# Two indexer units advanced together behind 13 products of ones, reversed queries for a small bias table, and h fetched four chunks ahead

## The chip, the core and the metric

The kernel runs on one core of a Trainium2 chip. A core has five engines that run their own instruction streams and meet at semaphores: TensorE (PE, matrix products; its weight loads are listed apart as PEld), VectorE (DVE), ScalarE (ACT), GpSimd (POOL) and SyncE (SP, which here only issues transfers). Products read SBUF and write PSUM, which has eight banks of 128 x 512 fp32. The metric is the device time of one execution in microseconds (us).

## The reference, cut to what matters

Two layers act on x (256 tokens, width 2048). Layer 0 multiplies the normalised x by one wide weight matrix whose columns feed an RG-LRU recurrence and a sparse attention; layer 1 is a gated MLP. After each layer a gated per-layer embedding is added to the residual h.

```python
# layer 0, attention: an indexer scores every key for every query, 64 keys are kept
s_h = relu(einsum('bqhd,bsd->bqhs', iqb, ik))              # 16 indexer heads of 64
score = einsum('bqhs,bqh->bqs', s_h, iwb) * idx_scale      # iw: a weight per query and head
score = where(key_pos < (q_pos // 64 + 1) * 64, score, -inf)
_, sel = top_k(score, 64)
logits = einsum('bqgrd,bqkgd->bqgrk', qg, kg) * att_scale  # 16 heads of 128, 4 kv heads
bias = rel_table[t5_bucket(sel - q_pos)]                   # depends on key - query and head alone
probs = softmax(logits + bias)
o = einsum('bqgrk,bqkgd->bqgrd', probs, vg)
# each layer
h = h + mix
h = h + sigmoid(rms_norm(h) @ w_gate) * (p_i @ w_pe)
```

## The kernel before

Weights come from HBM in chunks of 128 rows by two k tiles by 512 columns (368 for the indexer). For each chunk SP issues a load (L147), ACT rounds the weights to `hi` (L155), DVE computes the rest `lo = raw - hi` (L156), and PE multiplies: the activations are split the same way, and each k tile and half of the tokens takes three products in fp32r, hi by xh, lo by xh and hi by xl (L189 to L191), so 12 products to a chunk. `unit` makes the chunks of one 512-column block; `spair` and `half_pair` make blocks with seven instead of eight multiplications (tiles U, V, W, Z), whose chunks are half as long.

`program` appends all chunks to one list and walks it. At chunk j it issues loads (at most 13 raw buffers) and splits up to three chunks ahead (`feed`), then chunk j's products, and then `advance` lets every background task go one step, up to its next `yield`. A task does what lies around the products: it takes finished PSUM tiles, transposes, scores, scans. A scheduler then sets each engine's final order from what tasks and chunks issue; each engine executes its own in order. `spawn(task, n)` delays a task by n steps.

Names that the change and the prediction touch:

- `fm` (L437): four 128 x 128 transpositions on PE, `nc.tensor.transpose` with an identity; used with tiles iqt (indexer queries), qt (queries), kt, ht, ybt and more. In `head_pair` three more a head transpose the softmax numerators (tile pt, L735).
- `idx_task`, `iq_task`: take the indexer's three 368-column units (key `ik`, weight `iw`, 16 query heads `iq`), then per step two products pairs `sc` (L589), relu on ACT and weighted sums on DVE; `topk` makes the mask.
- `bias_table`: a product makes a 16 x 384 table of head by (key - query); ACT writes it 128 times, each row shifted by one, to an HBM scratch of 3 MB (L493). `head_pair` reads a 128 x 2 x 256 tile of it (L695).
- `fetch` and `add_h_task`: h lies in HBM between the gate of layer 0 and layer 1; when a block of layer 1's output projection ("y") is complete, `add_h_task` issues the fetch (L917), and adds a step later (L926), and `to_acts` transposes the sum (ht) a step after that.
- the lead of `program`: loads and splits of the first three chunks and of all eight x tiles before the walk.

The lines most spoken of:

```python
437  def fm(self, a0, a1, name="fm"):
443      self.nc.tensor.transpose(pt[...], x[:, k * 128:(k + 1) * 128], self.ident)
571  nc.scalar.activation(iq, pt, AF.Copy)             # iqT
735  nc.tensor.transpose(pt[:, o:o + 128], L[h][:, c:c + 128], self.ident)
744  nc.tensor.matmul(po[:, o0:o0 + 128], PT[h][:, 0:128], self.v[0][:, kv], start=True, stop=True)
917  self.nc.sync.dma_start(h, self.hd[c, t])
926  self.nc.vector.tensor_tensor(hs[t], ps[t], hs[t], op=OP.add)
1057 nc.tensor.matmul(pm[:, s], self.ws[c][:, i], self.ov[c, t][:, s], start=True, stop=True)
```

Of the kernel before, what the change touches and what calls it, by code (L numbers as in the profile page):

```python
# [27 lines left out]
T = 256  # L28
# [3 lines left out]
H = 16  # L32
# [37 lines left out]
class Chunk:  # L70
    def __init__(self, ap, cols, mm, half=False):
        self.ap, self.cols, self.mm, self.half = ap, cols, mm, half
        self.prev = self.next = self.raw = self.hl = None
        self.spawn = []
# [7 lines left out]
class Trunk:  # L82
# [259 lines left out]
    def half_stage(self, key, prev, acts, task, *args, before=None, lead=4, tail=3):  # L342
# [4 lines left out]
        def rest(i):  # L347
            def f(ps):
                st["h%d" % i] = []
                for t in range(2):  # L350
# [10 lines left out]
                            [self.post(task, c, *args) for c in (0, 1)], first)  # L361
        ss = ss[:10] + pre(1) + [None, None] + ss[10:12] + pre(0) + [None, None] + ss[12:]
# [14 lines left out]
        self.chunks += cs  # L377

# [58 lines left out]
    def fm(self, a0, a1, name="fm"):  # L437

        pt = self.pa(name)
        with self.tc.issue_after(self.last_mm.ins):  # L440
            for k in range(2):
                for t, x in ((0, a0), (1, a1)):
                    self.nc.tensor.transpose(pt[:, k * T + t * 128:k * T + (t + 1) * 128],  # L443
                                             x[:, k * 128:(k + 1) * 128], self.ident)
# [21 lines left out]
    def consts(self):  # L466
# [3 lines left out]
        self.ident = self.kept([128, 128], "ident")  # L470
        nc.gpsimd.dma_start(self.ident, a["ident"])
# [3 lines left out]
        nc.scalar.activation(warm, self.mhalf, AF.Tanh)  # L475
        self.r = {}

    def bias_table(self):
# [7 lines left out]
        with self.tc.issue_after(self.last_mm.ins):  # L486
            nc.tensor.matmul(ps[:H, :N_BUCKET_COLS], rel, oh, start=True, stop=True)
        sb = self.kept([H, N_BUCKET_COLS], "bt")
        nc.scalar.activation(sb, ps[:H, :N_BUCKET_COLS], AF.Copy)

        bd = self.bias_d = self.dram.tile([H, 128, 512], F32, name="bias_d")
        yield
        nc.scalar.dma_start(bass.AP(tensor=bd.tensor, offset=bd.offset, ap=[[128 * 512, H], [513, 128], [1, 383]]),  # L493
                            sb[:, None, :383].to_broadcast([H, 128, 383]))
# [31 lines left out]
    def idx_task(self, i, ps):  # L526
# [3 lines left out]
        if i == 0:  # L530
# [16 lines left out]
            with self.tc.issue_after(self.last_mm.ins):  # L547
                for t in range(2):
                    nc.tensor.transpose(pt[:, t * 128:(t + 1) * 128], ikd[t], self.ident)
            self.ik = self.t([128, T], name="ik")  # L550
# [13 lines left out]
    def iq_task(self, j):  # L564
# [4 lines left out]
        pt = self.fm(self.iq[j // 2][0][:, o:o + T], self.iq[j // 2][1][:, o:o + T], "iqt")  # L569
# [31 lines left out]
    def topk(self):  # L601
        nc = self.nc
        sc = self.score
        nc.vector.memset(sc[0:64, 192:256], OUT_OF_RANGE)
        nc.vector.memset(sc[0:64, 320:384], OUT_OF_RANGE)
# [62 lines left out]
    def q_task(self, g, ps):  # L668
# [5 lines left out]
        rq = self.kept([128, 2, 4], "rq")  # L674
        nc.vector.tensor_scalar(rq, ss, 128 * EPS, None, op0=OP.add)
        nc.gpsimd.tensor_tensor(self.flat(rq), self.flat(rq), self.mhalf, op=OP.pow)
        self.rq[g] = rq
        qT = []
        for p in range(2):
            pt = self.fm(qs[0][:, p * T:(p + 1) * T], qs[1][:, p * T:(p + 1) * T], "qt")  # L680
# [3 lines left out]
        yield  # L684
        yield from self.until("mask", "k", "v", "bias")
# [4 lines left out]
    def head_pair(self, g, p, qT):  # L690
# [4 lines left out]
        nc.gpsimd.dma_start(bt, bass.AP(tensor=bd.tensor, offset=bd.offset + h0 * 128 * 512 + 127,  # L695
                                        ap=[[512, 128], [128 * 512, 2], [1, T]]))
# [31 lines left out]
        rc = self.sm([128, 4])  # L728
        nc.vector.reciprocal(rc, sm)
        for i, t in ((0, 1), (1, 0)):  # L730
            nc.vector.tensor_scalar(rc[:, 2 * i:2 * i + 2], rc[:, 2 * i:2 * i + 2], self.rth("x", t), None, op0=OP.mult)
        for h in range(2):
            pt = self.pa("pt")
            for o, c in ((0, 256), (128, 0), (256, 128)):
                nc.tensor.transpose(pt[:, o:o + 128], L[h][:, c:c + 128], self.ident)  # L735
            x = self.t([128, 384], name="PT")
            nc.scalar.activation(x, pt[:, :384], AF.Copy)
            PT.append(x)
        yield
# [172 lines left out]

    def fetch(self, c):
# [6 lines left out]
    def add_h_task(self, c, layer, ps):  # L920
        if layer == 1:
            self.fetch(c)
            yield
# [189 lines left out]
    def program(self):  # L1113
# [9 lines left out]
        for i in range(3):  # L1123
            self.put(self.unit([a["idx_w"][i, :, o * 736:(o + 1) * 736] for o in range(8)], xs,
                               self.post(self.idx_task, i), n=368))
# [43 lines left out]

# [155 lines left out]
```

## Time and profile before

| | us |
|---|---|
| median of 3 timed runs | 1246.75 (1245.07 to 1247.82) |
| the profiled execution | 1248.01 |
| its span (first to last instruction) | 1246.2 |
| PE busy | 1227.4 (98%) |
| DVE busy | 944.3 (76%) |
| ACT busy | 785.0 (63%) |

The profile comes from one execution. Busy time of PE counts a product until its result is out, so products overlap in it; how fast PE goes is read from start to start. The rest of the profiled execution, 1.8 us, lies around the span. All numbers of the rows below are from this execution.

### The profile page before, as it was taken

To read this page: it belongs to the slowest core of one execution; us is meant where nothing else is said; L and a number is where in the kernel's file an instruction comes from. 1 tells how busy PE (TensorE), PEld (TensorE's weight loads), DVE (VectorE), ACT (ScalarE), POOL (GpSimd) and SP (SyncE) were. 2 spreads that over 40 slices of the span, in tenths; PEclk is the share of its full clock that TensorE was granted. 3 is DMA by queue.
4 is the path that set the end of the run, shared out by engine and by line. 5 is a ranking of instruction groups with operands and counts; after the bars stand their busy time and mean duration, and the time that the engine had idled before them with its cause. 6 is when DMAs were issued, how large, how long until landed. Compare 5 with 4: busy or idle time off the path is not lost.

```text
span 1246.2 us, 16543 instructions
## 1 busy us (share of the span) xinstructions
PE 1227.4 (98%) x5780; PEld 1023.8 (82%) x5780; DVE 944.3 (76%) x1487; ACT 785.0 (63%) x1099; POOL 147.4 (12%) x178
## 2 busy tenths in 40 slices
PE   7999999999999999999999999999999999999998
PEld 7978887888888888888888888788888888887886
DVE  6779658786677778775568877887899778677865
ACT  6755546664477878863466776676765656565753
POOL 0001131412000001000110110032112000100100
PEclk9999999999999999999999999999999999999999
DMA  9997997636546555576787798889999965986961
GB/s 345 253 249 231 299 219 240 227 128 199 183 157 201 172 186 177 178 239 216 188 246 250 187 291 281 225 241 271 274 274 277 279 222 156 244 267 203 261 186 43
DMA packets 82868, 279.31 MB, mean 224 GB/s; under 512 B 9264, under 2 KB 11968, under 8 KB 82784
## 3 DMA queue, kind: packets, MB, share of 16 engines
q1 hardware_dynamic: 66672, 225.18, 52.0%
q0 software_dynamic: 14048, 49.94, 21.2%
q10 hardware_dynamic: 2064, 3.14, 1.9%
q8 instruction: 45, 0.74, 0.2%
q14 instruction: 39, 0.32, 0.1%
HBM read 270.89 MB, written 7.33 MB: 223 GB/s over the span
## 4 chain that ended last, share of the span: by engine, by line
PE 89%; DMA 5%; DVE 3%; issue 2%; ACT 1%; SPq 0%; POOL 0%; DVEq 0%; ACTq 0%
PE pg L191 22%; PE pg L189 22%; PE pg L190 22%; DMA bias_d<-bt 3%; PE U L229 1%; PE U L231 1%; PE U L230 1%; DVE lo L156 1%; ACT hi L155 1%; PE ht L443 1%; PE Z L230 1%; PE Z L229 1%; PE Z L231 1%; PE V L230 1%; PE U L290 1%
## 5 line engine op out<-in xcount | busy, mean ns | idle before, releaser
L156 DVE TENSOR_TENSOR lo<-raw,hi 128x1024 fp32r<-128x1024 f32 (+1 forms) x492 | 587.6, 1212 | 201.5 <-ACT hi L155 197.2
L155 ACT ACTIVATE hi<-raw 128x1024 fp32r<-128x1024 f32 (+1 forms) x492 | 511.5, 1048 | 350.2 <-PE pg L191 256.0
L189 PE MATMUL pg<-hi,xh 128*128 128x512 f32 (+1 forms) x1376 | 536.9, 390 | 6.8 <-ACT xh L426 6.3
L190 PE MATMUL pg<-lo,xh 128*128 128x512 f32 (+1 forms) x1376 | 532.0, 387 | 0.5 <-DVE lo L156 0.5
L191 PE MATMUL pg<-hi,xl 128*128 128x512 f32 (+1 forms) x1376 | 531.9, 387 | 0.5 <-DVE xl L427 0.4
L189 PEld LDWEIGHTS pg<-hi,xh 128*128 128x128 f32 x1376 | 259.5, 189 | 57.6 <-ACT xh L426 6.9
L191 PEld LDWEIGHTS pg<-hi,xl 128*128 128x128 f32 x1376 | 259.0, 188 | 51.7 <-DVE xl L427 1.6
L190 PEld LDWEIGHTS pg<-lo,xh 128*128 128x128 f32 x1376 | 259.5, 189 | 49.1 <-DVE lo L156 1.0
L160 POOL DMA_DIRECT2D raw<-in_w7h x32 | 27.7, 866 | 357.3 <-DMA raw<-in_w 197.5
L160 POOL DMA_DIRECT2D raw<-in_w x48 | 41.8, 892 | 203.7 <-DVE lo L156 110.6
L426 ACT ACTIVATE xh<-ht,cols 128x256 fp32r<-128x256 f32 x48 | 22.0, 469 | 19.1 <-DVE xl L427 11.9
L803 POOL TENSOR_TENSOR tt<-tt,tg 128x512 f32<-128x512 f32 x8 | 10.3, 1294 | 183.1 <-ACT tt L801 164.3
L229 PE MATMUL U<-hi,xh 128*128 128x512 f32 x72 | 29.0, 403 | 0.0
L231 PE MATMUL U<-lo,xh 128*128 128x512 f32 x72 | 28.1, 390 | 0.0
L230 PE MATMUL U<-hi,xl 128*128 128x512 f32 x72 | 28.1, 390 | 0.0
L427 DVE SCALAR_TENSOR_TENSOR xl<-ht,cols,xh 128x256 fp32r<-128x256 f32 x48 | 22.6, 481 | 5.7 <-ACT xh L426 5.6
L725 ACT ACTIVATE L<-L,s 128x256 f32<-128x256 f32 (+1 forms) x32 | 14.3, 448 | 15.5 <-DVE s L719 14.8
L434 DVE TENSOR_TENSOR xl<-s,xh 128x512 fp32r<-128x512 f32 x32 | 22.0, 687 | 1.9 <-ACT xh L433 1.9
L433 ACT ACTIVATE xh<-s 128x512 fp32r<-128x512 f32 x32 | 19.9, 622 | 4.8 <-DVE s L414 4.7
L717 DVE SCALAR_TENSOR_TENSOR L<-lg,rq,bm 128x256 f32<-128x256 f32 (+1 forms) x32 | 12.0, 410 | 14.4 <-POOL bm L702 12.4
L829 DVE SCALAR_TENSOR_TENSOR xc<-xat,cols,xc 128x255 f32<-128x255 f32 (+2 forms) x48 | 22.2, 477 | 0.5
L231 PE MATMUL V<-lo,xh 128*128 128x512 f32 x48 | 18.8, 391 | 0.5 <-DVE lo L156 0.5
(310 smaller groups left out, 1346.9 us busy)
## 6 DMA issues: line engine op xcount, KB each, us to landing
raw<-in_w SPq DMA_DIRECT2D x356, 512.0 KB, 5.0
raw<-in_w POOLq DMA_DIRECT2D x48, 512.0 KB, 8.7
raw<-in_w7h POOLq DMA_DIRECT2D x32, 512.0 KB, 7.1
raw<-in_w7h SPq DMA_DIRECT2D x24, 512.0 KB, 4.4
raw<-in_idx_w SPq DMA_DIRECT2D x24, 368.0 KB, 7.4
raw<-in_pe_w SPq DMA_DIRECT2D x8, 512.0 KB, 6.0
bias_d<-bt ACTq DMA_DIRECT2D x1, 3064.0 KB, 35.9
x<-in_xT SPq DMA_DIRECT2D x8, 256.0 KB, 7.3
```

Source lines behind the costliest of these rows:

```text
L155: nc.scalar.activation(hi[:, :c.cols], raw, AF.Copy)
L156: self.last_lo = nc.vector.tensor_tensor(lo[:, :c.cols], raw, hi[:, :c.cols].bitcast(F32), op=OP.subtract)
L160: nc.gpsimd.dma_start(c.raw, c.next.ap, accum_op=OP.add)
L189: self.nc.tensor.matmul(ps, xh, wh, start=(c == order[0] and k == 0), stop=False)
L190: self.nc.tensor.matmul(ps, xh, wl, start=False, stop=False)
L191: self.last_mm = self.nc.tensor.matmul(ps, xl, wh, start=False, stop=(c == order[-1] and k == 1))
L229: nc.tensor.matmul(st[b], ah, wh, start=new and k == 0, stop=False, skip_group_check=True)
L230: nc.tensor.matmul(st[b], al, wh, start=False, stop=False, skip_group_check=True)
L231: self.last_mm = nc.tensor.matmul(st[b], ah, wl, start=False, stop=(c == order[3] and k == 1), skip_group_check=True)
L426: nc.scalar.activation(hi[:, s], src[:, s], AF.Copy, scale=g)
L427: nc.vector.scalar_tensor_tensor(lo[:, s], src[:, s], g, hi[:, s].bitcast(F32), op0=OP.mult, op1=OP.subtract)
L829: nc.vector.scalar_tensor_tensor(xc[:, s, k:], xa[:, s, :T - k], col(C_CW + (3 - k) * 16 + f), xc[:, s, k:], op0=OP.mult, op1=OP.add)
```

## The change

- Lead: a tile of ones is set on DVE, and 13 products of it (128 x 512, fp32r) stand at the head of PE's order. Loads are queued x tile by x tile with two weight chunks each; ten are issued ahead; x tiles are split as the walk comes to them.
- Indexer: the chunks of its first two units alternate, so that both use the same x tile one after the other; the third unit follows. x norm and x sums start later (13 and 19 steps).
- Queries in reverse: indexer queries, queries and softmax numerators go through a plain product with a reversed identity instead of a transposition. The weights `iw` and the sums of squares `ss` and of the softmax `sm` go through small products with it, so that they come in the same order. The table is then written once (24 KB), and read with a step of one element from partition to partition.
- Fetch of h: for "y", the loads are a task of their own, started four chunks before the block's last chunk; `add_h_task` adds at once.

```diff
@@ -361,2 +361,4 @@
                             [self.post(task, c, *args) for c in (0, 1)], first)
+        cs[7].ends, ss[11].ends, ss[13].ends, cs[-1].ends = 2, 1, 0, 3
+        mark = len(self.chunks)
         ss = ss[:10] + pre(1) + [None, None] + ss[10:12] + pre(0) + [None, None] + ss[12:]
@@ -377,2 +379,6 @@
         self.chunks += cs
+        if key == "y":
+            for i in range(mark, len(self.chunks)):
+                if self.chunks[i].ends is not None:
+                    self.chunks[i - 4].spawn.append(lambda c=self.chunks[i].ends: self.fetch_task(c))
 
@@ -436,3 +442,4 @@
 
-    def fm(self, a0, a1, name="fm"):
+    def fm(self, a0, a1, name="fm", flip=False):
+
 
@@ -442,4 +449,8 @@
                 for t, x in ((0, a0), (1, a1)):
-                    self.nc.tensor.transpose(pt[:, k * T + t * 128:k * T + (t + 1) * 128],
-                                             x[:, k * 128:(k + 1) * 128], self.ident)
+                    o = pt[:, k * T + t * 128:k * T + (t + 1) * 128]
+                    x = x[:, k * 128:(k + 1) * 128]
+                    if flip:
+                        self.nc.tensor.matmul(o, x, self.flip, start=True, stop=True)
+                    else:
+                        self.nc.tensor.transpose(o, x, self.ident)
         return pt.rearrange("p (a b) -> p a b", a=2)
@@ -469,4 +480,5 @@
         nc.sync.dma_start(self.cols, a["cols"])
-        self.ident = self.kept([128, 128], "ident")
-        nc.gpsimd.dma_start(self.ident, a["ident"])
+        both = self.kept([128, 256], "ident")
+        nc.gpsimd.dma_start(both, a["ident"])
+        self.ident, self.flip = both[:, 0:128], both[:, 128:256]
         self.mhalf = self.kept([128, 8], "mhalf")
@@ -475,2 +487,7 @@
         nc.scalar.activation(warm, self.mhalf, AF.Tanh)
+        ones = self.t(name="ones")
+        nc.vector.memset(ones, 1.0)
+        ps = self.pa("warm")
+        for i in range(13):
+            nc.tensor.matmul(ps, ones[:, 0:128].bitcast(F32R), ones.bitcast(F32R), start=True, stop=True)
         self.r = {}
@@ -487,9 +504,8 @@
             nc.tensor.matmul(ps[:H, :N_BUCKET_COLS], rel, oh, start=True, stop=True)
-        sb = self.kept([H, N_BUCKET_COLS], "bt")
+        sb = self.t([H, N_BUCKET_COLS], name="bt")
         nc.scalar.activation(sb, ps[:H, :N_BUCKET_COLS], AF.Copy)
 
-        bd = self.bias_d = self.dram.tile([H, 128, 512], F32, name="bias_d")
+        self.bias_d = self.dram.tile([H, N_BUCKET_COLS], F32, name="bias_d")
         yield
-        nc.scalar.dma_start(bass.AP(tensor=bd.tensor, offset=bd.offset, ap=[[128 * 512, H], [513, 128], [1, 383]]),
-                            sb[:, None, :383].to_broadcast([H, 128, 383]))
+        nc.scalar.dma_start(self.bias_d, sb)
         self.done.add("bias")
@@ -549,2 +565,5 @@
                     nc.tensor.transpose(pt[:, t * 128:(t + 1) * 128], ikd[t], self.ident)
+                nc.tensor.matmul(pt[:, T:T + 2 * IH], self.flip, self.flat(self.iw), start=True, stop=True)
+            self.iw = self.kept([128, 2, IH], "iwf")
+            nc.scalar.activation(self.flat(self.iw), pt[:, T:T + 2 * IH], AF.Copy)
             self.ik = self.t([128, T], name="ik")
@@ -568,3 +587,3 @@
         o = (j % 2) * T
-        pt = self.fm(self.iq[j // 2][0][:, o:o + T], self.iq[j // 2][1][:, o:o + T], "iqt")
+        pt = self.fm(self.iq[j // 2][0][:, o:o + T], self.iq[j // 2][1][:, o:o + T], "iqt", True)
         iq = self.t([128, 2, T], name="iqT")
@@ -603,4 +622,4 @@
         sc = self.score
-        nc.vector.memset(sc[0:64, 192:256], OUT_OF_RANGE)
-        nc.vector.memset(sc[0:64, 320:384], OUT_OF_RANGE)
+        nc.vector.memset(sc[64:128, 192:256], OUT_OF_RANGE)
+        nc.vector.memset(sc[64:128, 320:384], OUT_OF_RANGE)
         for rnd in range(8):
@@ -673,9 +692,5 @@
         self.head_sums(qs, ss)
-        rq = self.kept([128, 2, 4], "rq")
-        nc.vector.tensor_scalar(rq, ss, 128 * EPS, None, op0=OP.add)
-        nc.gpsimd.tensor_tensor(self.flat(rq), self.flat(rq), self.mhalf, op=OP.pow)
-        self.rq[g] = rq
         qT = []
         for p in range(2):
-            pt = self.fm(qs[0][:, p * T:(p + 1) * T], qs[1][:, p * T:(p + 1) * T], "qt")
+            pt = self.fm(qs[0][:, p * T:(p + 1) * T], qs[1][:, p * T:(p + 1) * T], "qt", True)
             x = self.t([128, 2, T], name="qT")
@@ -684,2 +699,9 @@
         yield
+        ps = self.pa("rq")
+        with self.tc.issue_after(self.last_mm.ins):
+            nc.tensor.matmul(ps[:, 0:8], self.flip, self.flat(ss), start=True, stop=True)
+        rq = self.kept([128, 2, 4], "rq")
+        nc.vector.tensor_scalar(self.flat(rq), ps[:, 0:8], 128 * EPS, None, op0=OP.add)
+        nc.gpsimd.tensor_tensor(self.flat(rq), self.flat(rq), self.mhalf, op=OP.pow)
+        self.rq[g] = rq
         yield from self.until("mask", "k", "v", "bias")
@@ -694,4 +716,4 @@
         bd = self.bias_d
-        nc.gpsimd.dma_start(bt, bass.AP(tensor=bd.tensor, offset=bd.offset + h0 * 128 * 512 + 127,
-                                        ap=[[512, 128], [128 * 512, 2], [1, T]]))
+        nc.gpsimd.dma_start(bt, bass.AP(tensor=bd.tensor, offset=bd.offset + h0 * N_BUCKET_COLS,
+                                        ap=[[1, 128], [N_BUCKET_COLS, 2], [1, T]]))
         lg, bm, L, PT = [], [], [], []
@@ -727,6 +749,2 @@
         yield
-        rc = self.sm([128, 4])
-        nc.vector.reciprocal(rc, sm)
-        for i, t in ((0, 1), (1, 0)):
-            nc.vector.tensor_scalar(rc[:, 2 * i:2 * i + 2], rc[:, 2 * i:2 * i + 2], self.rth("x", t), None, op0=OP.mult)
         for h in range(2):
@@ -734,3 +752,5 @@
             for o, c in ((0, 256), (128, 0), (256, 128)):
-                nc.tensor.transpose(pt[:, o:o + 128], L[h][:, c:c + 128], self.ident)
+                nc.tensor.matmul(pt[:, o:o + 128], L[h][:, c:c + 128], self.flip, start=True, stop=True)
+            if h == 1:
+                nc.tensor.matmul(pt[:, 384:388], self.flip, sm, start=True, stop=True)
             x = self.t([128, 384], name="PT")
@@ -738,2 +758,6 @@
             PT.append(x)
+        rc = self.sm([128, 4])
+        nc.vector.reciprocal(rc, pt[:, 384:388])
+        for i, t in ((0, 1), (1, 0)):
+            nc.vector.tensor_scalar(rc[:, 2 * i:2 * i + 2], rc[:, 2 * i:2 * i + 2], self.rth("x", t), None, op0=OP.mult)
         yield
@@ -912,2 +936,6 @@
 
+    def fetch_task(self, c):
+        self.fetch(c)
+        yield
+
     def fetch(self, c):
@@ -920,5 +948,2 @@
     def add_h_task(self, c, layer, ps):
-        if layer == 1:
-            self.fetch(c)
-            yield
         hs = self.h[c]
@@ -1122,5 +1147,5 @@
         xs = lambda: self.xs
-        for i in range(3):
-            self.put(self.unit([a["idx_w"][i, :, o * 736:(o + 1) * 736] for o in range(8)], xs,
-                               self.post(self.idx_task, i), n=368))
+        idx = [self.unit([a["idx_w"][i, :, o * 736:(o + 1) * 736] for o in range(8)], xs,
+                         self.post(self.idx_task, i), n=368) for i in range(3)]
+        self.put(sum(map(list, zip(idx[0], idx[1])), []), idx[2])
         wu = lambda acts, task, *args, **kw: self.put(self.wunit(acts, self.post(task, *args), **kw))
@@ -1169,17 +1194,17 @@
 
+        def split_x(j):
+            if j < PAIRS and j not in self.xs:
+                self.xs[j] = self.split(x[j], self.cols[:, C_NG + 2 * j:C_NG + 2 * j + 2])
+
         with self.tc.manual_schedule():
             self.consts()
-            self.issue_load(0)
-            load_xt(0)
-            self.issue_load(1)
-            load_xt(1)
-            self.issue_load(2)
-            for j in range(2, PAIRS):
-                load_xt(j)
-            self.next_load = 3
             for j in range(PAIRS):
-                g = self.cols[:, C_NG + 2 * j:C_NG + 2 * j + 2]
-                if j in (0, 1, 3):
-                    self.feed(-1, {0: 1, 1: 2, 3: 3}[j])
-                self.xs[j] = self.split(x[j], g)
+                load_xt(j)
+                if j < 5:
+                    self.issue_load(2 * j)
+                    self.issue_load(2 * j + 1)
+            self.next_load = 10
+            for j in range(3):
+                split_x(j)
+                self.feed(-1, min(2 * j + 2, 5))
 
@@ -1204,4 +1229,4 @@
 
-        self.spawn(x_norm(), 8)
-        self.spawn(x_sums(), 16)
+        self.spawn(x_norm(), 13)
+        self.spawn(x_sums(), 19)
         self.spawn(self.bias_table(), 8)
@@ -1215,2 +1240,3 @@
                 self.spawn(mk())
+            split_x((j + AHEAD + 1) // 2)
             self.feed(j)
...
```

In the order that each engine executes, the change shows at three places. At the head of PE's order (pg are the units' PSUM tiles, hi and lo a chunk's weights, xh and xl an x tile), before:

```order
L189 MATMUL pg_184<-hi_113,xh_117 128x368
L190 MATMUL pg_184<-lo_114,xh_117 128x368
L191 MATMUL pg_184<-hi_113,xl_118 128x368
L189 MATMUL pg_184<-hi_113,xh_117 128x368
L190 MATMUL pg_184<-lo_114,xh_117 128x368
L191 MATMUL pg_184<-hi_113,xl_118 128x368
```

and now:

```order
L492 MATMUL warm_87<-ones_85 128x512 x13
L189 MATMUL pg_176<-hi_143,xh_137 128x368
L189 MATMUL pg_177<-hi_143,xh_137 128x368
L189 MATMUL pg_190<-hi_147,xh_137 128x368
L190 MATMUL pg_176<-lo_144,xh_137 128x368
L191 MATMUL pg_176<-hi_143,xl_138 128x368
L189 MATMUL pg_176<-hi_143,xh_137 128x368
L190 MATMUL pg_176<-lo_144,xh_137 128x368
```

A product of the second unit's chunk (hi_147) now stands third, ahead of the first that reads lo. 

ACT's order where the indexer's tiles are taken (ik and iqT feed the first sc products, pg_344 and pg_345 hold the second unit, pg_542 and pg_543 the third), before:

```order
L551 ACTIVATE ik_520<-ikt_517 128x256
L529 ACTIVATE iq_326<-pg_344 128x144
L529 ACTIVATE iq_327<-pg_345 128x144
L406 ACTIVATE xe_564<-x_87,cols_77 128x256
L155 ACTIVATE hi_613<-raw_480 128x736
L571 ACTIVATE iqT_577<-iqt_572 128x512
```

and now:

```order
L568 ACTIVATE iwf_641<-ikt_637 128x32
L570 ACTIVATE ik_643<-ikt_637 128x256
L439 ACTIVATE xh_663<-s_631 128x512
L545 ACTIVATE iq_495<-pg_542 128x368
L545 ACTIVATE iq_496<-pg_543 128x368
L590 ACTIVATE iqT_672<-iqt_667 128x512
```

The copy of iqT now stands behind two copies that read the third unit's finished tiles.

SP's order at the last two blocks of "y" (hr are the fetched tiles of h, raw the weights), before:

```order
L147 DMA raw_10640<-in_w 128x1024
L917 DMA hr_10340<-hd_7283 128x512
L917 DMA hr_10342<-hd_7285 128x512
L147 DMA raw_10659<-in_w7h 128x1024
L147 DMA raw_10673<-in_w 128x1024
L147 DMA raw_10703<-in_w 128x1024
L917 DMA hr_10468<-hd_7417 128x512
L917 DMA hr_10470<-hd_7419 128x512
```

and now:

```order
L147 DMA raw_10643<-in_w 128x1024
L945 DMA hr_10311<-hd_7318 128x512
L945 DMA hr_10313<-hd_7320 128x512
L147 DMA raw_10662<-in_w7h 128x1024
L945 DMA hr_10379<-hd_7452 128x512
L945 DMA hr_10381<-hd_7454 128x512
L147 DMA raw_10675<-in_w 128x1024
```

The last block's two loads moved past two weight loads, to directly behind the first load after the other block's.

## Rows read from the trace of the kernel before

**Rows 1.** The page: the span, and busy time of each engine with its instructions.
```profile
span 1246.2 us, 16543 instructions
...
PE 1227.4 (98%) x5780; PEld 1023.8 (82%) x5780; DVE 944.3 (76%) x1487; ACT 785.0 (63%) x1099; POOL 147.4 (12%) x178
```
**Rows 2.** Waits of PE: waiter <- awaited: us in total, times, longest.
```profile
PE pg L189 <- ACT xh L426: 6.3, 2, 6.1
PE sc L589 <- ACT iqT L571: 2.4, 1, 2.4
PE ht L443 <- DVE hr L926: 1.9, 3, 1.5
...
```
**Rows 3.** Groups of PE: line, out<-in, shape, xcount | busy us, mean ns | idle before.
```profile
L735 PE MATMUL pt<-ident,L 128*128 128x128 f32 x48 | 6.5, 272 | 0.0
L744 PE MATMUL o<-v,PT 128*128 128x128 f32 x32 | 6.3, 277 | 0.4 <-ACT PT L737 0.4
...
L443 PE MATMUL qt<-ident,q 128*128 128x128 f32 x24 | 3.1, 272 | 0.0
L443 PE MATMUL iqt<-ident,iq 128*128 128x128 f32 x16 | 2.4, 272 | 0.0
```
**Rows 4.** Timeline of PE around one head pair's transpositions: start us, us, what.
```profile
175.94 0.82 PE L735 MATMUL pt<-ident,L 128*128 128x128 f32 x6
...
176.83 0.40 PE L230 MATMUL U<-hi,xl 128*128 128x512 f32 x1
177.06 0.40 PE L231 MATMUL U<-lo,xh 128*128 128x512 f32 x1
```
**Rows 5.** Timeline of PE around four plain fp32 products of layer 1.
```profile
948.25 1.05 PE L1057 MATMUL mix<-v,ws 128*128 128x128 f32 x8
...
949.37 0.40 PE L230 MATMUL U<-hi,xl 128*128 128x512 f32 x1
```
**Rows 6.** Line 735: weight loads, ns min/median/max, first and last start.
```profile
L735 PEld LDWEIGHTS pt<-ident,L x48: 138/140/144, 175.7 to 335.0; 128*128 128x128 f32 x48
```
**Rows 7.** Timeline of PE at the start.
```profile
6.07 0.68 PE L189 MATMUL pg<-hi,xh 128*128 128x368 f32 x1 [6.07 <-ACT xh L426]
...
11.30 0.51 PE L190 MATMUL pg<-lo,xh 128*128 128x368 f32 x1
11.60 0.51 PE L191 MATMUL pg<-hi,xl 128*128 128x368 f32 x1
...
17.09 0.33 PE L191 MATMUL pg<-hi,xl 128*128 128x368 f32 x1
17.26 0.33 PE L189 MATMUL pg<-hi,xh 128*128 128x368 f32 x1
```
**Rows 8.** Timeline of ACT at the start.
```profile
5.50 0.91 ACT L426 ACTIVATE xh<-x,cols 128x256 fp32r<-128x256 f32 x2
6.55 0.82 ACT L155 ACTIVATE hi<-raw 128x736 fp32r<-128x736 f32 x1
...
8.95 0.91 ACT L426 ACTIVATE xh<-x,cols 128x256 fp32r<-128x256 f32 x2 [1.57 <-DMA x<-in_xT]
```
**Rows 9.** The chain that ended last, 38 to 80 and 1136 us: start us, us, what.
```profile
38.97 35.94 DMA bias_d<-bt
74.98 3.58 DMA raw<-in_w
...
1136.43 5.93 DMA hr<-hd
```
**Rows 10.** Timeline of ACT, 62 to 66 us: the third unit's copies.
```profile
64.28 0.96 ACT L529 ACTIVATE iq<-pg 128x368 f32<-128x368 f32 x2
```
**Rows 11.** Timeline of PE, 192 to 194 us.
```profile
192.88 0.40 PE L230 MATMUL V<-hi,xl 128*128 128x512 f32 x1
193.81 0.50 PE L231 MATMUL V<-lo,xh 128*128 128x512 f32 x1 [0.53 <-DVE lo L156]
```
**Rows 12.** Groups of DVE at line 926.
```profile
L926 DVE TENSOR_TENSOR hr<-h,hr 128x512 f32<-128x512 f32 x4 | 2.8, 693 | 1.6 <-DMA hr<-hd 1.5
```

More of the change, by code (lines that the diff above doesn't have):

```diff
@@ L72, in __init__ @@
         self.ap, self.cols, self.mm, self.half = ap, cols, mm, half
-        self.prev = self.next = self.raw = self.hl = None
+        self.prev = self.next = self.raw = self.hl = self.ends = None
         self.spawn = []
@@ L1168, in load_xt @@
             x.append(t)
+        def split_x(j):
+            if j < PAIRS and j not in self.xs:
+                self.xs[j] = self.split(x[j], self.cols[:, C_NG + 2 * j:C_NG + 2 * j + 2])
         with self.tc.manual_schedule():
             self.consts()
-            self.issue_load(0)
-            load_xt(0)
-            self.issue_load(1)
-            load_xt(1)
-            self.issue_load(2)
-            for j in range(2, PAIRS):
-                load_xt(j)
-            self.next_load = 3
-            for j in range(PAIRS):
-                g = self.cols[:, C_NG + 2 * j:C_NG + 2 * j + 2]
-                if j in (0, 1, 3):
-                    self.feed(-1, {0: 1, 1: 2, 3: 3}[j])
-                self.xs[j] = self.split(x[j], g)
+            for j in range(PAIRS):
+                load_xt(j)
+                if j < 5:
[5 more added lines that the diff above has]
+                self.feed(-1, min(2 * j + 2, 5))
         def x_norm():
@@ L1306, in _layout @@
         "pT": c(np.asarray(i["p"])[:, 0].reshape(2, T, 2, 128).transpose(0, 3, 2, 1)),
-        "ident": np.eye(128, dtype=np.float32),
+        "ident": np.concatenate([np.eye(128, dtype=np.float32), np.eye(128, dtype=np.float32)[::-1]], axis=1),
         "onehot": _buckets(),
```

## The prediction

> **What bounds the kernel now.** I read four views. The page's first part comes first: PE is busy for 1227.4 of a span of 1246.2 us, and the next engine, DVE, for 944.3 [rows 1]. So a microsecond of product time counts in full, and one of DVE or ACT only where PE waits for it. The waits of PE come second: 6.1 us until its first product, and later 2.4 us before an indexer product, 1.9 us in three waits for h, and smaller ones [rows 2]. All that this change can win lies in those waits and in the slow clock of the start. Third, the start of PE's timeline: products of 368 columns begin 0.306 us apart at 11.30 and 11.60, and 0.168 apart later (17.09, 17.26) [rows 7]. 368 columns in 0.306 us are 1.2 GHz, the lower level; from about 12 us on it is 2.4. Fourth, the groups of PE, for what is exchanged: transpositions and plain products.
>
> **The sum is made against the profiled execution, 1248.0 us (span 1246.2 and 1.8 around it).** It lies 1.3 above the median of 1246.75, so the result goes onto the median.
>
> **Reversal, the large term.** 96 transpositions become plain fp32 products with the reversed identity: 16 iqt, 32 qt (24 and 8 of another name) and 48 pt [rows 3]. A transposition is one record: L735 has 48 records for 8 head pairs x 2 heads x 3. A plain fp32 product is two: L744 has 32 for 8 x 2 products [rows 3]. Their pace: six transpositions start at 175.94, the second product behind them at 176.83; less one normal step of 0.23 that is 0.66 us, 0.110 each [rows 4]. Four plain products (eight records) start at 948.25, the second product behind at 949.37; less 0.23 that is 0.89, 0.223 each [rows 5]. Same shape, same type. So each flip costs 0.113 us more, 96 of them 10.8 us. They stand in PE's order where PE has almost no idle time, so nothing hides them. The operands of a flip are fp32, not fp32r, and the call is a plain one, so I see no reason for a single record.
>
> The Trainium skill (TensorE: Matmul & The Clock Gate, Terms) goes further against this edit: its transpose mode is 4 times faster for FP32. Here a plain product costs 2.0 times a transposition, so the measurement decides; by the page's ratio a flip would cost 0.33 more and the sum 20.9 us more. It stays as a rival.
>
> **Small products.** 13 more with 32, 8 or 4 columns (iw one, ss four, sm eight), 26 records. The trace has none so narrow. Each must still load 128 x 128 weights, for which a record shows 0.138 to 0.144 us [rows 6]: at most 26 x 0.14 = 3.6. The other end is nothing, if their loads hide behind the products before. The nearest row is the 128-column record, 0.111 us: I take 26 x 0.111 = 2.9. The same page (Wait — 56ns, not 53.3ns?) has a floor of about 25 ns for small products; that would be 0.65 us, inside my bounds, and no row here shows it.
>
> **Start.** Before, 38 products had begun ahead of 17.09; from there PE runs evenly, at 0.168. It is as if it had started at 17.09 - 38 x 0.168 = 10.7 at full speed. Now the ones: DVE sets 128 x 512, at most 0.69 us (an addition of that size [rows 12]), so the products begin at about 1.4; at the lower level 512 columns take 512/368 x 0.306 = 0.43, thirteen 5.6, to 7.0. Before, the clock rose some 5.9 us after the first product (6.07 to about 12); that again gives 7.3. Data: the x tile and first weights now stand second and third in the queue. The second weights stand fourth, with the same bytes ahead as before, and their split could begin by 6.55; after the x split (0.91 for both halves) and the first weights' it starts at about 6.6 and takes 0.82 [rows 8]. So PE's third product, which needs it, begins at about 7.4, and full speed counts from 7.4 - 2 x 0.168 = 7.1. That is 3.6 earlier. The second x tile again stands fifth, and landed by 8.95 [rows 8]; its weights and their splits (another 0.91, 0.82 and DVE's) come at about 11 to 12, and PE wants them at 7.1 + 24 x 0.168 = 11.1. For that I take 0.6 off: -3.0, between -3.6 and -1.5. From then on two chunks use one x tile (4.0 us of products), and ACT and DVE need less for it.
>
> **Bias table.** The write held the queues from 38.97 for 35.94 us, the next weights landed 3.58 us later, and the chain from there ends in the wait of 2.4 us of sc for iqT [rows 2, 9] (2.6 from start to start). With 24 KB this goes: -2.6; at worst another late copy takes its place, 0.
>
> **ACT's new order.** There is one. iqT now stands behind two copies of the third unit, of which the second needs the unit's last product, and sc stands directly behind that product. Result out (0.33, the length of a product in rows 7), then a copy of about 0.47 (0.96 for two, [rows 10]) and iqT's own, about as long, less one normal step of 0.17: +1.3, from 0 (if the scheduler's order gives ACT its slack elsewhere) to +1.8.
>
> **Fetch.** The last block's h was issued at 1136.43 and landed 5.93 us later [rows 9]; DVE's additions waited 1.5 [rows 12], PE 1.9 in three waits [rows 2], each about 0.2 more from start to start, 2.5. Fetched earlier, and with the sum one step sooner, these go; what is late next is the last block's transposition and split. -2.5; -1.5 if only the longest goes, -3.0 if those splits, now a step sooner, save PE some wait too. SP issues as many DMAs as before; only their places change.
>
> **Near 193.** PE waits there for DVE's lo (0.93 from start to start instead of 0.23, 0.7 lost [rows 11]) and soon after 0.4 for a copy [rows 3]. The flips just ahead lengthen PE's work by 0.7 per head pair and give DVE that time: -0.9, from -1.1 to 0. The reciprocal that now waits for PE stands on DVE behind the lo of three chunks that PE has not begun (by the order), 3 x 12 x 0.23 = 8 us of cover; without this cover each of its 8 waits would show on PE.
>
> **Sum.** 10.8 + 2.9 - 3.0 - 2.6 + 1.3 - 2.5 - 0.9 = +6.0: 1254.0 against 1248.0, and 1252.7 on the median. All small terms at their good ends: 10.8 - 3.6 - 2.6 - 3.0 - 1.1 = +0.5. At their bad ends: 10.8 + 3.6 - 1.5 + 1.8 - 1.5 = +13.2.
>
> **Rivals.** (a) The gains are near their good ends and the small products hide: between 0 and +2.5, 1246.8 to 1249.2. For: all small terms have honest room; against: they would have to agree. (b) The clock does not rise with the ones. PE may wait between the last of them and the third real product, just when the rise is due, and then the first 5.9 us of real products run at half speed: 3.0 us lost, +9.0, 1255.7. For: my times of the two lie within half a microsecond. Against: the gap between the two would be under half a microsecond. The Trainium skill's page (TensorE: Matmul & The Clock Gate, What's actually happening) says that the number of slow products differs from run to run; the trace has one start and can't show it. (c) Faster: a product with the reversed identity goes at a transposition's pace, one record of 0.110. Then 10.8 falls away: -4.8, 1241.9. It decides as soon as a flip costs less than 0.05 us above a transposition. For it speaks only that transpositions and flips move the same bytes; against it every plain fp32 product of the trace. (d) The page's factor of 4: 1252.7 + 20.9 = 1273.6.
>
> **Chances.** Forecast 66 in 100, by itself 1249.8 to 1256; (a) 17; (b) 10; (c) 6; (d) 1. 0.2%, 2.5 us, is about what a measurement of this kernel can tell from no change. Faster: (c) and, for what I can't see, one more, 7. Same: the rest of (a) and the lowest part of the forecast, 18. Slower: 75. The range leaves out (c), (d), the best part of (a) and the worst of (b): 1247.5 to 1257.
>
> **What would show it.** Two records for each flip, iqt 32, qt 64, pt 96, 0.111 apart: the large term; 48 pt would refute it. Products of 0.168 apart by 7.5 us: the start; 0.306 beyond 8 would be (b). No wait before sc near 85, but one of about 1.3 at the first sc. No wait of DVE for hr. The forecast is wrong if the indexer's and heads' stretch (75 to 350 us) does not become longer by some 10 us.

## The result, and the profile after

Changed kernel: 1258.89 us (median of 4, 1258.15 to 1259.16), before 1246.45 (4 runs): ratio 1.0099, interval 1.0081 to 1.0116. Slower, as forecast, but by 12.4 us where 6.0 were forecast (1252.7, range 1247.5 to 1257.0). The profiled execution of after lies 0.7 under its median and that of before 1.6 over its own (1.3 over the median of three in the table of before); so their spans, from which the terms below are read, lie 10.1 apart, 2.3 less than the medians.

The first part of the page answers to [rows 1]: PE is busy for 15.5 us more, the other engines for as long as before.

```profile
span 1256.3 us, 16823 instructions
...
PE 1242.9 (99%) x5915; PEld 1041.2 (83%) x5915; DVE 943.9 (75%) x1488; ACT 785.8 (63%) x1100; POOL 144.8 (12%) x178
```

The waits of PE, against [rows 2]: the wait of sc near 85 us is gone and that for hr is down to 0.3, but one of 3.6 us stands first that was not there. It was not in the forecast.

```profile
PE ikt L565 <- issue: 3.6, 1, 3.6
PE warm L492 <- DVE ones L489: 1.4, 1, 1.4
PE sc L608 <- ACT iqT L590: 1.1, 1, 1.1
PE pg L189 <- ACT hi L155: 1.0, 2, 0.6
...
PE ht L455 <- DVE hr L951: 0.3, 1, 0.3
```

"issue" names no releaser, so the timeline of all engines around it has to (start us, us, engine, line). The last x fetch lets ACT go at 55.83 and DVE at 56.67; the sums, POOL's power rx, the scaled key ikd on DVE and at last ikt on PE follow one upon the other, 3.8 us in all. PE had come to ikt at 55.9.

```profile
55.71 0.33 PE L189 MATMUL pg<-hi,xh 128*128 128x368 f32 x1
55.83 0.63 ACT L894 ACTIVATE junk<-xn 128x512 f32<-128x512 f32 x1 [1.49 <-DMA xn<-in_x]
...
56.67 0.69 DVE L1217 SCALAR_TENSOR_TENSOR xn<-xn 128x512 f32<-128x512 f32 x1 [0.89 <-DMA xn<-in_x]
...
57.83 0.16 DVE L463 TENSOR_SCALAR s<-s 128x2 f32<-128x2 f32 x1
...
58.14 0.73 POOL L465 TENSOR_TENSOR rx<-s,mhalf 128x2 f32<-128x2 f32 x1 [54.53 <-DVE s L463]
58.91 0.25 DVE L558 TENSOR_SCALAR ikd<-ikd,rx 128x64 f32<-128x64 f32 x1 [0.67 <-POOL rx L465]
...
59.62 0.32 PE L565 MATMUL ikt<-ident,ikd 128*128 128x128 f32 x1 [3.58 <-issue]
```

The same timeline of before. Here, too, the chain ended just as PE came: ikd began at 43.27, ikt at 43.95. There was no slack to give away.

```profile
40.53 0.63 ACT L870 ACTIVATE junk<-xn 128x512 f32<-128x512 f32 x1 [1.59 <-DMA xn<-in_x]
...
42.51 0.73 POOL L454 TENSOR_TENSOR rx<-s,mhalf 128x2 f32<-128x2 f32 x1 [38.89 <-DVE s L452]
...
43.27 0.26 DVE L542 TENSOR_SCALAR ikd<-ikd,rx 128x64 f32<-128x64 f32 x1 [0.92 <-POOL rx L454]
...
43.95 0.33 PE L549 MATMUL ikt<-ident,ikd 128*128 128x128 f32 x1
```

Stretches of after (us, busy time and instructions by engine, then PEclk, DMA share, GB/s): PE works for 0.12 of 3.7 us, and in the 3.5 us that follow, busy all the time, it has 0.51 of the clock.

```profile
50.00:56.00 6.00, 6.00 (x36) 5.73 (x35) 3.38 (x5) 3.15 (x7) 0.00 (x0) 1.00 0.99 364
56.00:59.70 3.70, 0.12 (x2) 0.11 (x2) 2.36 (x12) 2.84 (x5) 1.00 (x2) 1.00 0.88 301
59.70:63.20 3.50, 3.50 (x16) 3.50 (x17) 3.50 (x7) 1.25 (x4) 0.00 (x0) 0.51 0.31 99
```

The groups of PE that answer to [rows 3]: 96 records for the 48 flips of pt, and the small products.

```profile
L753 PE MATMUL pt<-ident,L 128*128 128x128 f32 x96 | 12.0, 274 | 0.0
L453 PE MATMUL qt<-ident,q 128*128 128x128 f32 x48 | 5.8, 275 | 0.0
...
L453 PE MATMUL iqt<-ident,iq 128*128 128x128 f32 x32 | 5.4, 315 | 0.0
...
L755 PE MATMUL pt<-s,ident 128*128 128x4 f32 x16 | 2.3, 212 | 0.0
...
L702 PE MATMUL rq<-s,ident 128*128 128x8 f32 x8 | 1.1, 213 | 0.0
```

### The profile page after: what moved, and what is told of

Same layout as the page of the kernel before. It is cut to its first block, busy times and chain, and to the rows that moved or that the text cites. A ratio compares the mean times of both kernels' runs of the same rounds, so it can differ in the third digit from the quotient of the medians.

```text
span 1256.3 us, 16823 instructions
## 1 busy us (share of the span) xinstructions
PE 1242.9 (99%) x5915; PEld 1041.2 (83%) x5915; DVE 943.9 (75%) x1488; ACT 785.8 (63%) x1100; POOL 144.8 (12%) x178
## 4 chain that ended last, share of the span: by engine, by line
PE 97%; DVE 1%; issue 1%; DMA 0%; ACT 0%; SPq 0%; DVEq 0%; ACTq 0%
PE pg L189 24%; PE pg L191 24%; PE pg L190 24%; PE U L229 1%; PE U L231 1%; PE U L230 1%; PE Z L229 1%; PE V L229 1%; PE Z L230 1%; PE Z L231 1%; PE U L289 1%; PE V L230 1%; PE U L290 1%; PE V L231 1%; PE U L291 1%; PE ht L455 1%
## 5 line engine op out<-in xcount | busy, mean ns | idle before, releaser
L432 ACT ACTIVATE xh<-ht,cols 128x256 fp32r<-128x256 f32 x48 | 22.0, 469 | 17.2 <-DVE xl L433 10.6
L827 POOL TENSOR_TENSOR tt<-tt,tg 128x512 f32<-128x512 f32 x8 | 10.3, 1292 | 184.2 <-ACT tt L825 165.5
L229 PE MATMUL Z<-hi,xh 128*128 128x512 f32 x48 | 19.0, 395 | 0.0
```

What stands on the lines that cost most here:

```text
L229: nc.tensor.matmul(st[b], ah, wh, start=new and k == 0, stop=False, skip_group_check=True)
L432: nc.scalar.activation(hi[:, s], src[:, s], AF.Copy, scale=g)
```

## The experiments

Theory T: the large term is right, and the miss is the wait at ikt with the half clock behind it; the x norm (13 chunks in, not 8) comes too late for the place at which ikt stands in PE's order. All times are medians; the ratio is to the kernel before on the same chip.

**norm8**
```
-        self.spawn(x_norm(), 13)
-        self.spawn(x_sums(), 19)
+        self.spawn(x_norm(), 8)
+        self.spawn(x_sums(), 16)
```


> The changed kernel with one thing undone: the x norm starts 8 chunks in and its sums 16, as before, not 13 and 19. Theory T (the late norm makes the key's transposition ikt wait for rx, and TensorE's clock falls behind that wait): the wait of 3.7 us ahead of ikt goes, the granted clock stays at 1.0 from the warm products to the end, which gives back another 1.7; 1258.9 - 5.4 = 1253.5, between 1252.5 and 1254.7. Rival R1 (the x fetches then stand among the indexer's weight fetches, and PE waits for those weights instead): 1256.5 or more, with a wait of a product pg for hi or lo between 25 and 45 us. Rival R2 (the norm isn't the cause; the wait comes with the new place of the key's task): no change, 1258.9.

1259.81, 1.0111 (1.0097 to 1.0124): nothing won, T's number missed. R1 is nearest, by another way than the one it names: ACT's squares of xn stand ahead of its splits, ACT waits for the fetch, and PE for the splits behind. ikt still waits (1.2 and 0.4), and the granted clock is 0.50 from 33.0 to 36.4 us, behind the first place, and 0.51 from 50.0 to 53.5, behind the second. Waits of norm8, 22 to 37 us:

```profile
ACT junk L894 <- DMA xn<-in_x: 10.0, 2, 9.1
...
PE pg L189 <- ACT hi L155: 2.4, 1, 2.4
```

So an earlier norm is no remedy: the fetch comes later than its place in ACT's order allows. And as ikt waits 1.6 with the norm back at 8 chunks, the late norm by itself isn't shown to be the whole cause.

**key_later**
```
-            yield 2
+            yield 8
             pt = self.pa("ikt")
```


> The changed kernel with the key's transposition put 8 instead of 2 steps behind its scaling: ikt stands 32 products (6.8 us) further on in PE's order, and the queries' first transposition and sc move with it. Norm, fetches and start are untouched. Theory T (ikt only stands too early for rx, whose chain takes its own time): no wait at ikt, the granted clock stays at its upper level, 3.7 + 1.7 us less: 1253.5, at best 1252.3 if the wait of sc for iqT (1.1) goes too. Rival R1 (the fetches bound the first 60 us; without the pause at ikt PE runs into weights that have not landed): the wait turns up at products pg for hi between 50 and 90 us, 1256.5 or more.

1254.18, 1.0063 (1.0048 to 1.0077). The profiled execution is 5.4 us shorter than that of after, as T has it, but it is the fastest of its six; the medians lie 4.7 apart, and 3.9 with those of key_later_again below. No wait at ikt, no wait at pg in its place (R1 falls), and the clock holds:

```profile
56.00:63.00 7.00, 7.00 (x36) 5.96 (x34) 6.32 (x23) 5.49 (x11) 1.00 (x2) 1.00 0.58 203
```

The other executions agree on the clock: the mean over the execution is 0.997 or 0.998 in all four of after, and 0.999 or 1.0 in all six of key_later. So the wait at ikt and the half clock behind it are the largest part of the miss. Why rx is late there this does not show.

**flip_as_transpose**
```
-    self.nc.tensor.matmul(o, x, self.flip, start=True, stop=True)
+    self.nc.tensor.transpose(o, x, self.flip)      # and so for pt
```


> The changed kernel with the 96 products with the reversed identity issued as TensorE transpositions with the same reversed identity as operand; the 13 small products stay plain. Theory T (plain fp32 products cost two records of 0.111 us where a transposition costs one of 0.109): iqt 16, qt 32 and pt 48 records, 96 x 0.113 = 10.8 us less, 1248.1, between 1247.0 and 1249.2. Rival R2 (with a reversed identity the pace is that of a plain product whatever the mode): 1258.9. Rival R3 (the faster flips give ACT and DVE less time between, and waits like that near 193 us come back): 1249.5 to 1251.

1247.28, 1.0010 (1.0001 to 1.0019): 11.6 under after, in T's range. The flips halve their records, and a transposition with the reversed identity does reverse. R3's sign shows, though not its number: waits near 193 us are back (pt for L 0.6, V for lo 0.5), with the clock at 0.53 from 196.0 to 199.6.

```profile
L753 PE MATMUL pt<-ident,L 128*128 128x128 f32 x48 | 6.8, 273 | 0.6 <-ACT L L747 0.6
```

**transpose_and_key_later**: both edits.

> The changed kernel with both: the 96 flips as transpositions with the reversed identity, and the key's transposition 8 steps behind its scaling. Theory T: 1247.3 measured with the first alone, less 3.8 for the wait at ikt and 1.7 for the clock: 1241.8, between 1240.5 and 1243.5; the waits near 193 us stay. Rival R1 (the wait turns up at later weights): 1246 to 1248.

1246.56, 0.9998 (0.9989 to 1.0007). In the traces it ends 3.1 us ahead of flip_as_transpose, not 5.5, and by the medians 0.7: sc now waits 1.1 for iqT, which it had not there. T's size is missed; R1's number comes, its place does not: no weights are waited for. The rest of the shortfall stays open.

**no_ones, key_later_no_ones, key_later_again, no_ones_same_chip**
```
-        for i in range(13):
-            nc.tensor.matmul(ps, ones[:, 0:128].bitcast(F32R), ones.bitcast(F32R), start=True, stop=True)
```


> The changed kernel without the 13 products of ones. Theory T (PE gets ahead at the start only to wait at ikt for an rx that comes at its own time): the real products begin at about 7 us at the lower clock and PE is some 3 us behind by 15 us; the wait at ikt shrinks by as much, from 3.7 to about 0.8, and the clock may not fall behind it (-1.7): between 1257.0 and 1259.5. Rival R4 (the start's gain is kept to the end, and the wait at ikt is no shorter): +2.9, 1261.8.

1258.74, 1.0094: the ones are worth nothing here, as T has it, though the wait at ikt shrank from 3.75 to 2.9 only (from start to start), and the clock fell for longer in the profiled execution (0.50 from 61.0 to 70.8 us).

> The changed kernel with the key's transposition 8 steps behind its scaling and without the 13 products of ones. Theory T (the start's gain is real, and was only spent in the wait at ikt): with that wait out of the way the ones count again, so this is slower than key_later by the 2.4 us that the traces of no_ones and of the changed kernel lie apart before 55 us: 1254.2 + 2.4 = 1256.6, between 1255.5 and 1257.7. Rival R4 (the ones are worth nothing in any case, since weights or splits set the pace behind them): 1254.2.

> The kernel of key_later once more, on the same chip as the next, since the two medians came from two chips. It is the base of that comparison: 1254.2, between 1253 and 1255.5, and 1.0063 of the kernel before.

> The kernel of key_later_no_ones beside key_later_again. Theory T (the start's gain lasts once nothing waits at ikt): 2.4 us slower than key_later_again, at least 1.2. Rival R4 (the ones are worth nothing): within 0.8 us of it.

Without the ones against with them: 1254.07 (1.0068) against 1254.18 (1.0063), measured at different times (on one chip by its number, not on two as is said above), and 1253.82 (1.0061) against 1255.01 (1.0069), measured together. T fails: the ones gain nothing. R4 is nearer, but its reason is not shown: past 10 us neither trace has a wait of more than 0.4 us for weights or splits. Its 0.8 is exceeded too, with the faster median on the side without ones; the intervals overlap. With the ones PE is 1.7 us ahead at 55 us; then sc waits for iqT, 1.7 us with them and 0.2 without, and in the profiled execution with them the clock falls behind that. Waits of key_later_again and its stretch behind, then the wait of no_ones_same_chip:

```profile
PE sc L608 <- ACT iqT L590: 1.7, 1, 1.7
```
```profile
73.60:77.00 3.40, 3.40 (x9) 2.61 (x9) 3.40 (x11) 1.49 (x4) 0.00 (x0) 0.50 0.83 292
```
```profile
PE sc L603 <- ACT iqT L585: 0.2, 1, 0.2
```

**head_alone**: of the change, the new start and the late norm only.

> The kernel before with the new start alone: the 13 products of ones, the first two indexer units k by k, the x tiles split as they are needed, the norm 13 and its sums 19 chunks in. Queries are not reversed, the bias table stays at 3 MB, h is fetched as before. Theory T: the start wins 2.9, the late norm costs 3.7 at ikt and 1.7 by the clock behind it, the wait for iqT stays at about 2: 1246.45 - 2.9 + 5.4 = 1249.0, between 1247.5 and 1250.5. Rival R2 (the wait at ikt comes with the reversed iw or the small table, not with the start): no wait at ikt, 1243.6.

1274.72, 1.0231: far over both. The norm's fetches now lie behind the 3 MB table's write, and ikt waits 22.1 us; and the squares again stand ahead of splits, so that pg waits 5.3 near 30 us. Waits of PE in head_alone; the timeline of its ACT shows the second:

```profile
PE ikt L554 <- issue: 22.1, 1, 22.1
PE pg L189 <- ACT hi L155: 6.1, 2, 5.3
```
```profile
22.56 0.80 ACT L155 ACTIVATE hi<-raw 128x736 fp32r<-128x736 f32 x1
34.05 0.63 ACT L875 ACTIVATE junk<-xn 128x512 f32<-128x512 f32 x1 [10.69 <-DMA xn<-in_x]
```

**head_late_table**
```
-        nc.scalar.dma_start(... ap=[[128 * 512, H], [513, 128], [1, 383]]) ...)
+        for r in range(0, 128, 16):
+            yield 3
+            nc.scalar.dma_start(... offset=bd.offset + r * 513, ap=[[128 * 512, H], [513, 16], [1, 383]]) ...)
-        self.spawn(self.bias_table(), 8)
+        self.spawn(self.bias_table(), 28)
```


> head_alone with the 3 MB table written in 8 pieces of 16 rows from chunk 28 on. The key's transposition stands 30 products earlier in PE's order than in the changed kernel. Theory T (the 22 us at ikt in head_alone were the x fetches behind the long write): the wait shrinks to the 3.7 us of the changed kernel or, as ikt stands 5 us earlier, to at most 8.8; with the clock behind it (1.7 to 5) that gives 1246.8 - 2.9 - 2.6 + 5.4 to 13.8 = 1246.7 to 1255.1, nearest 1250. Rival R7 (the late norm by itself costs those 22 us): 1270 or more.

1270.81, 1.0201. The number is R7's, the trace is not: ikt waits 2.0, so the long write was behind the 22 us. The time goes to pg near 30 us again (5.1) and, past 180 us, to heads that wait for the last pieces (6.5 and others).

**reversal_alone**

> The kernel before with the reversal alone: 96 plain products with the reversed identity, 13 small products and the 24 KB table; the start, the norm (8 chunks in) and the fetch of h as before. Theory T: + 10.8 for the flips, + 1.9 for the small products (24 of the 26 records of the changed kernel take some 0.07 each), - 2.6 for the wait of sc near 85 us and - 0.9 near 193: 1246.45 + 9.2 = 1255.7, between 1254.5 and 1257. Rival R1 (the reversal also makes the key's task late, through the table's place in ACT's order or through iw): + 3.7 and more, 1259.4. Rival R3 (the write of the table was not behind the wait near 85): 1258.3.

1258.60, 1.0092 (1.0076 to 1.0107): 2.9 over T's number, 0.8 under R1's. From 150 to 350 us it loses 10.7, like after (10.3); the waits for hr stay, and ikt waits 1.1 for ikd. So PE waits at ikt with the old start and the norm at 8 chunks too, which T had not; the rest of the 2.9 stays open. The reversal alone is as slow as the whole change.

**fetch_alone**

> The kernel before with the fetch of h four chunks ahead alone. Theory T: the waits of ht for hr go (1.9 us, 2.5 from start to start), nothing else moves: 1246.9 - 2.7 = 1244.2, between 1243.3 and 1245.4. Rival R5 (the fetches ahead delay the last block's weights, and PE waits for those): 1246 to 1248, with a wait for hi or lo between 1050 and 1160 us.

1244.80, 0.9981 (0.9972 to 0.9991): T, and the only version here that beats both kernels. Of the three waits for hr one is left:

```profile
PE ht L449 <- DVE hr L933: 0.5, 1, 0.5
```

**fetch_and_pieces, fetch_and_early_pieces, best_parts**: the table in pieces as above, with fetch_alone; then from chunk 14, two steps apart; then from chunk 28 with the new start and the later key.

> The kernel before with the early fetch of h and with the 3 MB bias table written in 8 pieces of 16 rows from chunk 28 on, its start and norm as before. Theory T (the single long write is behind the wait of sc near 85 us): 1244.8 - 2.6 = 1242.2, between 1241.2 and 1243.5. Rival R6 (the pieces cost weights their place elsewhere): 1244 to 1246.

> The kernel before with the early fetch of h and the 3 MB table in 8 pieces of 16 rows, from chunk 14 on and two steps apart, so that the last piece is issued by about 110 us instead of 164. Theory T (in fetch_and_pieces the first heads waited for the last pieces, and the pieces themselves cost little): the waits between 180 and 215 us go, the wait of sc near 85 shrinks from 2.6 to at most 1: 1244.8 - 1.6 to - 2.6 = 1242.2 to 1243.2. Rival R6 (pieces beside the indexer's and key's weights cost as much as the long write): 1244.5 to 1247.

> The kernel before with what paid: the new start (ones, two units k by k, norm 13 and sums 19 chunks in), the key's transposition 8 steps behind its scaling, h fetched four chunks ahead; nothing reversed. The 3 MB bias table is written in 8 pieces of 16 rows, three steps apart, from chunk 28 on. Theory T: 1246.8 - 2.9 (start) - 2.6 (wait of sc near 85) - 2.0 (fetch, as measured alone) + 1.0 (sc for iqT) = 1240.3, between 1238.8 and 1242.5. Rival R6 (each piece of the write delays the weights of its stretch, and PE waits for hi or lo between 80 and 170 us): 1243 to 1246.

1259.57 (1.0109), 1249.70 (1.0028), 1269.70 (1.0195): all three miss T. The wait of sc near 85 is gone in each, but in the first and third the first heads wait for the last piece (6.6 us), and in the second PE waits 4.4 us for a split, from 111.4 to 115.7: ACT has a copy of kT ahead of the splits that waits for PE and, through it, for the key's norm, so that the first hi starts at 109.25, and DVE has steps of the top-k ahead of its lo, which starts at 114.47. ikt waits 1.7 for ikd in the first two. The third waits 5.6 near 30 us, as head_alone does, and 5.2 for a split near 146. Waits of PE past 100 us in fetch_and_pieces, then in fetch_and_early_pieces (whole):

```profile
PE pg L189 <- DVE L L725: 6.6, 1, 6.6
PE pg L190 <- DVE lo L156: 3.9, 3, 2.3
```
```profile
PE pg L190 <- DVE lo L156: 4.9, 2, 4.4
```

**reversal_by_transposes**: the changed kernel with flips as transpositions, on the start of before.

> The changed kernel's reversal (with its flips as transpositions with the reversed identity, and the 24 KB table) and its early fetch of h on the start of before: no ones, indexer unit by unit, norm 8 and sums 16 chunks in. Theory T: 1244.8 (fetch alone) - 2.6 (wait of sc near 85) + 1.9 (small products) + 0 to 1.3 (ikt, as in reversal_alone) + 0 to 1 (waits near 193) = 1244.1 to 1246.4. Rival R8 (the waits near 193 us grow without the time that plain flips gave DVE, and the clock falls behind them): 1247 to 1249.

1246.16, 0.9997 (0.9989 to 1.0006): within T's range, and no gain over the kernel before; the waits near 193 us and at ikt (1.1) stand there.

## Why the prediction was wrong, step by step

Sums are times from one record's start to the next, by tile, in the two traces.

- **Reversal, 10.8: right.** pt 10.7 instead of 5.15, qt 6.8 instead of 3.2; with the 16 of iqt 10.9. flip_as_transpose gives it back whole. The factor of 4 (d) and the pace of a transposition (c) both fall: each flip has two records, and one of pt takes 0.111 us.
- **Small products, 2.9: 1.9.** I priced both records of a pair at 0.111. Of pt's and rq's pairs one record takes 0.11 and one 0.03: pt's 16 take 1.1, rq's 8 0.55.
- **Start, -3.0: right at its place, by luck in part, and worth nothing at the end.** Counted back at full speed PE starts at 7.8 instead of 10.7, 2.9 earlier. The clock rose at 5.2 (the ones begin 0.427 us apart up to 5.03, 0.23 apart from 5.32), not at 7.3, ahead of the first real product, so (b) falls. The 0.6 that I took off for the second x tile was lost elsewhere: the third product began at 8.06, not 7.4, and from there to ikt PE has no wait in the trace. But I let the gain run through to the end, on a stretch in which rx and iqT, and not PE, set when ikt and sc begin. no_ones_same_chip shows the gain spent.
- **The step that failed: the key's chain, from the x norm's fetches over rx to ikt, has no term in the sum.** The later norm is named in the change and stands at nothing without a reason. The part "ACT's new order" priced iqT behind two copies, and not the key ahead of it. The wait that came cost 3.75 us from start to start, and with the half clock behind it 5.4 (key_later; 4.7 by the medians). The delay of five chunks alone would not have shown it, for ikt moves with the norm: the key is scaled once rx is there, and ikt stands two steps behind that. In PE's order it went from behind 192 products of the units to behind 280, 14.8 us of work, and with the earlier start PE came to it 11.9 us later. What moved further are the fetches. SP issued the first x fetch 10.6 us later and the last 14.7 (in the rows: first and last start), and the last square of x began 15.3 us later (40.53 and 55.83):

```profile
L896 SPq DMA_DIRECT2D xn<-in_x x8: 327/328/906, 23.8 to 35.7; - x8
```
```profile
L920 SPq DMA_DIRECT2D xn<-in_x x8: 328/423/503, 34.4 to 50.4; - x8
```

  Between them SP's order has loads of weights, and these waited for DVE's lo of an earlier chunk, whose raw buffer they reuse: 0.2 us in before (23 to 37 us), 8.4 in after (30 to 51 us).

```profile
SPq L147 <- DVE lo L156: 0.2, 1, 0.2
```
```profile
SPq L147 <- DVE lo L156: 8.4, 6, 3.0
```

  How much of this is the late norm's and how much that of the loads that now run further ahead, no run separates: ikt also waits with the norm at 8 chunks, 1.6 with the new start (norm8), and with the old one 1.1 (reversal_alone) and 1.7 (fetch_and_pieces).
- **Bias table, -2.6: right.** The wait near 85 us is gone, also with the table in pieces; in the two ways tried of writing 3 MB in pieces, more was lost elsewhere than this wait gave.
- **ACT's new order, +1.3: 1.2.**
- **Fetch, -2.5: -2.7** between 1080 and 1180 us; alone 2.0 by the medians. It is not free of waits in every execution: that of key_later_again has 1.5 us for hr again.
- **Near 193, -0.9: -1.6.** No wait there; with transpositions in their place the waits return, so the flips' own length hid them, as I had it.

With these, 10.9 + 1.9 - 2.9 - 2.6 + 1.2 - 2.7 - 1.6 + 5.4 = 9.6 of the 10.1 between the spans. The bad end of the sum (+13.2) held the result by other terms than those that made it. And the sign that I had set for the forecast came, though the forecast failed: from 75 to 350 us the changed kernel loses 11.3, for the wait at ikt lies ahead of that stretch.

## What to carry to other kernels

Price every number that a change touches, above all a start delay: follow the moved work from its fetch to the first instruction of the bound engine that needs it, and compare with when that engine arrives; a chain that ended in time by a hair has no slack to give. Follow it through the queue that issues its fetches, too: the last one, moved by five chunks (10 us) in the program, was issued 14.7 us later, behind loads that waited for buffers. Time won ahead of a wait that data sets is not won. And where the reversed order is wanted, ask for it in the transposition that is there anyway: the same order as a plain fp32 product costs twice the time. (Here that brought the whole change level with the kernel before, and no further.)

## What the runs showed of the hardware that was not expected

A transposition's second operand may be the reversed identity: the output comes reversed, at the pace of any transposition (273 ns a record in flip_as_transpose, one record).

The clock does not fall behind every wait alike. Before and fetch_alone both wait 2.4 us for iqT near 85 us; behind it before keeps its clock, and fetch_alone has half for 3.5 us. The stretches of fetch_alone, then of before:

```profile
85.00:87.80 2.80, 0.40 (x5) 0.37 (x6) 2.80 (x9) 2.37 (x6) 0.00 (x0) 1.00 1.03 418
87.80:91.30 3.50, 3.50 (x14) 2.65 (x11) 3.50 (x6) 2.71 (x5) 0.00 (x0) 0.51 1.02 408
```
```profile
85.00:88.00 3.00, 0.59 (x4) 0.29 (x4) 3.00 (x9) 2.65 (x6) 0.00 (x0) 1.00 1.03 418
88.00:91.50 3.50, 3.50 (x21) 2.83 (x19) 3.50 (x7) 2.74 (x5) 0.00 (x0) 1.00 1.03 410
```

What decides it stays open. The mean clock goes with the time of an execution: of the 23 executions of the kernel before that were measured with fetch_alone, the four with a mean clock of 1.0 took 1244.3 to 1245.6 us, the eleven with 0.998 1245.4 to 1249.0. It is not the only reason why executions of one kernel lie apart: key_later's six, all at 0.999 or 1.0, go from 1252.8 to 1255.9.
